# A hybrid decoder layer on one core: keys' products over all rows, a later planned end of the conditioning's sums, 16x16 joins in four parts, and an earlier place for the RWKV output's weights

## The chip, the cores and the metric

The kernel runs on one core of one Trainium2 chip. The time is the device time of one execution in microseconds. The engines are named as in the profile: PE (TensorE, matrix products), DVE (VectorE), ACT (ScalarE), POOL (GpSimd) and SP (SyncE, which here issues most of the DMAs).

## The reference

One decoder layer in float32, D = 1024, 512 tokens, FF = 2816:

```python
for l in range(DEPTH):
    ada = (c @ w_ada[l] + b_ada[l])[:, None, :]
    sh1, sc1, gt1, sh2, sc2, gt2 = jnp.split(ada, 6, axis=-1)
    h = rms_norm(x, norm1_w[l]) * (1.0 + sc1) + sh1
    proj = h @ w_in[l]
    att_in, rwkv_in, gate_in = jnp.split(proj, [ATT_IN, ATT_IN + RWKV_IN], axis=-1)
    y_att = attention_mixer(att_in) @ w_att_out[l]
    y_rwkv = rwkv7_mixer(rwkv_in, ...) @ w_rwkv_out[l]
    g_att, g_rwkv = jnp.split(jax.nn.sigmoid(gate_in + b_gate[l]), N_BRANCHES, axis=-1)
    x = x + gt1 * ((g_att * y_att + g_rwkv * y_rwkv) @ w_o[l])
    h = rms_norm(x, norm2_w[l]) * (1.0 + sc2) + sh2
    x = x + gt2 * conv_ffn(h, w_up[l], conv_w[l], conv_b[l], w_down[l])
return rms_norm(x, norm_f_w)
```

`rwkv7_mixer` runs a recurrence over the tokens for each of 16 heads of 64 channels:

```python
def step(state, inp):
    r_t, w_t, k_t, v_t, aa_t, bb_t = inp
    sa = jnp.einsum('bhvk,bhk->bhv', state, aa_t)
    state = state * w_t[:, :, None, :] + sa[..., None] * bb_t[:, :, None, :] + v_t[..., None] * k_t[:, :, None, :]
    return state, jnp.einsum('bhvk,bhk->bhv', state, r_t)
```

## The kernel before, in words

**Number format.** Products of large matrices are made of three fp32r matmuls each (high by high, low by high, high by low halves). A weight block is loaded into a `raw` buffer by SP, cast by ACT into the high half (`whi`), and DVE subtracts it from the raw block for the low half (`wlo`). Nearly all of these matmuls are 128x512. The small products of the recurrence are plain fp32; the trace shows two records for each of them. All matmuls are issued by one helper at line 148.

**Two ways of ordering.** Up to the end of the recurrence, work is entered as tasks into a list scheduler (`Plan`, from line 47): each task has an engine, a planned time `us`, a planned `lag` until its result counts as there, a priority (smaller first) and room that it takes and gives. The plan is run while the kernel is built, and the order in which it starts the tasks is the order of instructions on each engine. So planned times decide only the order; the chip waits on semaphores for what is really ready. What follows (`rwkv_out`, `mix_out`, the FFN) stands in the order in which its code is written.

**Conditioning (lines 330 to 390).** `c @ w_ada` for the last four parts (gt1, sh2, sc2, gt2) is summed on DVE while PE computes the attention's projections: for each of eight row blocks SP loads 128x1024 weights into one of two `araw` buffers, and DVE multiplies by a column of c and adds to `acc` (line 347). After the eighth, PE adds over the partitions with the products `ada`: eight columns, or four pieces of 256.

**The recurrence (line 1060 on).** The heads are worked in four groups g of four heads (two pairs i), the tokens in chunks of C = 64, so there are NCH = 8 chunks for each group. Before the chain of a group, the inverse of each chunk's triangular matrix is made; for group 3 by `inverse16`, which works on 16x16 blocks: DVE makes their inverses, and PE joins two neighbours with two products (`half_pe(0)`, `half_pe(1)`, line 1679), each of 64 matmuls in 32x32 tiles of PE, and ACT copies each result (`half_out`). Then `chain(g)` (line 1745) goes through the chunks. On PE a chunk has `state` (tile `xy`: the old state `mbd` by `ar`, then the values `uv` by the matrices `gt`, the keys' products), `state_out` (tile `xo`), `solve` (`u`, from `xs`), `update` (`u` from `uv` and `bkt`), and `outs` (`xo` from `uv`). In a chunk of pair i, the 64 rows `R[i]` of `uv` hold that chunk's values; the rows `X[i]`, the other half, are filled by `solved`. The values are computed for two chunks at a time by `vals`: PE's `values` (centring, `u<-cen,v`) and two copies on ACT (`value`). The copies write only the rows and columns that hold values, the rest of a fresh `uv` is undefined until `solved`. There are two `uv` buffers. While the chain waits, PE works on tasks of lower priority: `pg` (branch gates), `pa` (attention output) and `pr` (first products of the RWKV output).

**Gates.** `early_gate(m)` computes one of the 16 gate blocks during or before the recurrence and stores it to DRAM; the blocks in `self.late` are computed later, as filling for the chain's waits.

**`rwkv_out` (line 2098).** Eight products `pr` of 24 matmuls follow each other (the first three had their first six row blocks done earlier). `first(3, ..)` and `first(4, ..)` load their weights into what will be the buffers of w_o's blocks 7 and 6. In each round m the kernel finishes product m, maybe loads a further block of RWKV output weights (`block`, appended to `ahead`), combines the gates, and loads block m of w_o (`load_wo`). Two `raw` buffers serve all these loads, and SP issues them in the order written.

Of the kernel before, what the change touches and what calls it, by code (L numbers as in the profile page):

```python
# [18 lines left out]
P = 128  # L19
# [109 lines left out]
class Layer:  # L129
# [198 lines left out]
    def ada_rest(self):  # L328
# [5 lines left out]
        for part, name in ((2, "gt1"), (3, "sh2"), (4, "sc2"), (5, "gt2")):  # L334
            d, prev = {}, None
            for k in range(KD):
                def load(k=k, d=d, part=part):
                    d["raw", k] = self.accp.tile([P, D], F32, tag="araw", name=self.n("araw"), bufs=2)
                    nc.sync.dma_start(d["raw", k], self.w_ada[0][k * P : (k + 1) * P, part * D : (part + 1) * D])

                def step(k=k, d=d):
                    raw, ck = d["raw", k], self.col["c"][:, k : k + 1]
                    if k == 0:
                        d["acc"] = self.accp.tile([P, D], F32, tag="acc", name=self.n("acc"), bufs=2)
                        nc.vector.tensor_scalar(d["acc"], raw, ck, 0.0, op0=ALU.mult, op1=ALU.add)
                    else:
                        nc.vector.scalar_tensor_tensor(d["acc"], raw, ck, d["acc"], op0=ALU.mult, op1=ALU.add)  # L347
                prio = W_ + self.bodies
                t = pl.add("DMA", 1.6, load, [self.wide], prio, take=("araw2",), lag=2.2, name="ada")
                prev = pl.add("DVE", 1.3 if k else 0.75, step, [t, prev], prio, take=() if k else ("acc2",),  # L350
                              give=("araw2",), name="ada")
                yield
# [688 lines left out]
    def rwkv(self, tail):  # L1041
# [32 lines left out]
        for g in range(4):  # L1074
# [3 lines left out]
            self.chain(g)  # L1078
        self.late = range(6, KD)
        for m in range(2 * KD):  # L1080
# [496 lines left out]
    def inverse16(self, g):  # L1577
# [100 lines left out]

        def half_pe(j):

            if j == 0:
                d["pe"] = self.cps.tile([P, 512], F32, tag="t", name=self.n("pe"))
            for y in range(16):
                for e, b, x in quads:
# [31 lines left out]
        for j in range(2):  # L1716
            t = pl.add("PE", 2.6, lambda j=j: half_pe(j), [t, ey], 0.5, take=() if j else ("t",), name="pe")
            tc = t = sca(0.42, lambda j=j: half_out(j), [t], 0.5, name="pe")
# [26 lines left out]
    def chain(self, g):  # L1745
# [18 lines left out]
        def values(c):  # L1764

            for n, i, x in ((0, 0, 0), (0, 1, 0), (1, 1, 1), (1, 0, 1)):
                r = 64 * (i ^ x)
                self.mm(d["u"][r : r + 64, n * P : n * P + P], prs[i]["v"][:, (c + x) * C : (c + x + 1) * C], self.cen,
                        n == 0, n == 1)

        def value(c, x):
            if x == 0:
                uvs[c] = cw.tile([P, 2, 256], F32, tag="uv", name=self.n("uv"), bufs=2)
            b = uvs[c].rearrange("p x (i n) -> p (x i) n", i=2)[64 * x : 64 * x + 64]
            nc.scalar.copy((b[:, 1:3] if x else b[:, 0:4:3]), d["u"][64 * x : 64 * x + 64, :].rearrange("p (i n) -> p i n", i=2))
# [7 lines left out]
        def vals(c):  # L1783
            t = pe(0.54, lambda: values(c), [start, last_uv])
            t = sca(0.38, lambda: value(c, 0), [t], C_, take=("uv",))
            uvd[c] = uvd[c + 1] = sca(0.38, lambda: value(c, 1), [t], C_)
        vals(0)
        for c in range(NCH):
# [9 lines left out]
            def state(c=c, s=s, gt=gt, R=R, X=X, ih=ih):  # L1798
# [4 lines left out]
                for i, h, cs, ci in ih:  # L1803
                    self.mm(xy[X[i], cs], gt(i, h, R[i], X[i]), s["uv"][R[i], ci], c == 0 and h == 0, h == 1)

# [43 lines left out]

            st = pe(0.6 if c else 0.33, state, [uvd[c], start] + mb, take=("xy",), name=f"xy{g}.{c}")  # L1850
            so_ = pe(0.33 if c else 0.0, state_out, [st], C_ + 0.01, take=("xo",), name="xo")
            x = sca(0.29, xs, [st], take=("xs",), give=("xy",))
# [245 lines left out]
    def rwkv_out(self, mpool, wpool, psp):  # L2098
# [16 lines left out]
        for m in range(KD):  # L2115
            w, pr = [ahead[0][x] for x in ("w", "pm")]
            ahead.pop(0)
            prod(w, pr, range(late if m < 3 else 0, KD))
            if 2 < m < KD - 2:
                ahead.append(block(m + 2))  # L2120
            t = self.tr_[m]
# [283 lines left out]
```

## Time and profile before

| what | value |
|---|---|
| runs (us) | 1217.01, 1217.9, 1211.57; median 1217.01 |
| profiled execution (us) | 1212.94 |
| its span (us) | 1211.2 |
| mean granted TensorE clock | 0.993 |
| PE busy, instructions | 97% of the span, 7456 matmul records |
| moved by DMA | 138.39 MB, 114 GB/s |

The span runs from the first to the last record; 1.74 us of the execution lie outside of it. The rest of the kernel by time: the norm and the first loads up to 40 us, the projections for attention and its conditioning sums to about 215 us, attention, the remaining projections and the recurrence to about 758 us, `rwkv_out` and `mix_out` to about 846 us, the FFN to the end. A matmul that stands behind another is pipelined, so the length of its record is longer than the distance to the next start; where a time per matmul is wanted, the difference of two starts is read.

### The profile page before, as it was taken

To read this page: it belongs to the slowest core of one execution; us is meant where nothing else is said; L and a number is where in the kernel's file an instruction comes from. 1 tells how busy PE (TensorE), PEld (TensorE's weight loads), DVE (VectorE), ACT (ScalarE), POOL (GpSimd) and SP (SyncE) were. 2 spreads that over 40 slices of the span, in tenths; PEclk is the share of its full clock that TensorE was granted. 3 is DMA by queue.
4 is the path that set the end of the run, shared out by engine and by line. 5 is a ranking of instruction groups with operands and counts; after the bars stand their busy time and mean duration, and the time that the engine had idled before them with its cause. 6 is when DMAs were issued, how large, how long until landed. Compare 5 with 4: busy or idle time off the path is not lost.

```text
span 1211.2 us, 18982 instructions
## 1 busy us (share of the span) xinstructions
PE 1170.6 (97%) x7456; PEld 945.9 (78%) x7456; DVE 737.5 (61%) x1248; ACT 542.3 (45%) x1014; POOL 108.6 (9%) x228
## 2 busy tenths in 40 slices
PE   4999998999999999999999999999999999999997
PEld 3788887889777776767787667788888888888886
DVE  5688862431668986855797564764566665652235
ACT  4475521622565555364636453444444444441223
POOL 4000000000000103122102222003000000000001
PEclk9999999999999999999999999999999999999999
DMA  9845871130143342422332335460233333332331
GB/s 316 257 131 171 280 223 56 53 91 18 23 135 95 83 115 78 122 74 75 87 97 86 117 94 159 155 209 18 70 97 94 104 88 105 89 117 93 103 122 70
DMA packets 168040, 138.39 MB, mean 114 GB/s; under 512 B 8753, under 2 KB 150155, under 8 KB 167951
## 3 DMA queue, kind: packets, MB, share of 16 engines
q1 hardware_dynamic: 167807, 136.93, 37.2%
q8 instruction: 58, 0.95, 0.3%
q14 instruction: 31, 0.25, 0.1%
q10 hardware_dynamic: 144, 0.26, 0.1%
HBM read 127.13 MB, written 10.04 MB: 113 GB/s over the span
## 4 chain that ended last, share of the span: by engine, by line
PE 81%; DVE 8%; DMA 6%; ACT 2%; issue 2%; SPq 0%; POOL 0%; POOLq 0%; DVEq 0%; ACTq 0%
PE u L148 22%; PE o L148 13%; PE v L148 7%; PE pg L148 7%; PE qk L148 6%; PE r L148 3%; DMA araw<-in_w_ada_dram 3%; PE k L148 3%; PE pa L148 2%; PE early L148 2%; PE po L148 2%; PE xy L148 2%; PE pr L148 2%; PE xo L148 2%; PE pt L151 1%
## 5 line engine op out<-in xcount | busy, mean ns | idle before, releaser
L194 DVE TENSOR_TENSOR wlo<-raw,whi 128x1024 fp32r<-128x1024 f32 x65 | 79.6, 1225 | 141.1 <-ACT whi L193 141.1
L148 PE MATMUL u<-h2hi,whi 128*128 128x512 f32 (+2 forms) x368 | 140.6, 382 | 0.0
L148 PE MATMUL u<-h2lo,whi 128*128 128x512 f32 (+2 forms) x368 | 140.6, 382 | 0.0
L148 PE MATMUL u<-h2hi,wlo 128*128 128x512 f32 (+2 forms) x368 | 140.5, 382 | 0.0
L1141 ACT CAST whi<-raw 128x1024 fp32r<-128x1024 f32 (+2 forms) x73 | 72.6, 994 | 119.6 <-PE qk L148 45.5
L193 ACT CAST whi<-raw 128x1024 fp32r<-128x1024 f32 x65 | 68.5, 1054 | 97.3 <-PE o L148 53.7
L1144 DVE TENSOR_TENSOR wlo<-raw,whi 128x1024 fp32r<-128x1024 f32 (+2 forms) x73 | 83.7, 1148 | 19.5 <-ACT whi L1141 19.3
L148 PEld LDWEIGHTS u<-h2hi,wlo 128*128 128x128 f32 x368 | 69.1, 188 | 13.2
L148 PEld LDWEIGHTS u<-h2hi,whi 128*128 128x128 f32 x368 | 69.1, 188 | 13.2
L148 PEld LDWEIGHTS u<-h2lo,whi 128*128 128x128 f32 x368 | 69.1, 188 | 13.2 <-POOL h2lo L405 0.2
L2231 DVE SCALAR_TENSOR_TENSOR u<-u,cols,u 128x511 f32<-128x511 f32 x88 | 65.7, 746 | 4.5 <-ACT u L2229 3.0
L148 PE MATMUL qk<-hhi,wlo 128*128 128x512 f32 x160 | 64.0, 400 | 0.0
L148 PE MATMUL qk<-hhi,whi 128*128 128x512 f32 x160 | 63.6, 398 | 0.0
L148 PE MATMUL qk<-hlo,whi 128*128 128x512 f32 x160 | 63.6, 397 | 0.0
L148 PE MATMUL o<-whi,fhi 128*128 128x512 f32 x144 | 56.1, 390 | 0.3 <-DVE u L2231 0.3
L148 PE MATMUL o<-whi,flo 128*128 128x512 f32 x144 | 56.0, 389 | 0.0
L148 PE MATMUL o<-wlo,fhi 128*128 128x512 f32 x144 | 56.0, 389 | 0.0
L148 PE MATMUL pg<-hlo,whi 128*128 128x512 f32 x128 | 52.0, 406 | 0.0
L148 PE MATMUL pg<-hhi,whi 128*128 128x512 f32 x128 | 51.6, 403 | 0.0
L148 PE MATMUL pg<-hhi,wlo 128*128 128x512 f32 x128 | 51.5, 403 | 0.0
L810 DVE CUSTOM_DVE_ANT_0 sm<-sc,m 128x256 f32<-128x256 f32 (+1 forms) x64 | 23.9, 404 | 37.6 <-PE sc L148 36.5
L347 DVE SCALAR_TENSOR_TENSOR acc<-araw,cols,acc 128x1024 f32<-128x1024 f32 x28 | 35.9, 1281 | 17.3 <-DMA araw<-in_w_ada_dram 17.1
(450 smaller groups left out, 2761.3 us busy)
## 6 DMA issues: line engine op xcount, KB each, us to landing
raw<-in_w_in_dram SPq DMA_DIRECT2D x62, 512.0 KB
raw<-in_w_up_dram SPq DMA_DIRECT2D x44, 512.0 KB
araw<-in_w_ada_dram SPq DMA_DIRECT2D x32, 512.0 KB
raw<-in_w_down_dram SPq DMA_DIRECT2D x22, 512.0 KB
araw<-in_w_ada_dram SPq DMA_DIRECT2D x32, 256.0 KB
wvraw<-in_w_in_dram SPq DMA_DIRECT2D x20, 256.0 KB
raw<-in_w_rwkv_out_dram SPq DMA_DIRECT2D x8, 512.0 KB
raw<-in_w_o_dram SPq DMA_DIRECT2D x8, 512.0 KB
```

The lines of the kernel that those rows point to most:

```text
L148: return self.nc.tensor.matmul(out, lhsT, rhs, start=start, stop=stop)
L151: self.nc.tensor.matmul(out, in_, self.ident[: in_.shape[0], : in_.shape[0]], is_transpose=True, start=start, stop=stop,)
L193: self.nc.scalar.copy(hl[0], raw)
L194: (lo_eng or self.nc.vector).tensor_tensor(hl[1], raw, hl[0], op=ALU.subtract)
L347: nc.vector.scalar_tensor_tensor(d["acc"], raw, ck, d["acc"], op0=ALU.mult, op1=ALU.add)
L810: nc.vector.tensor_tensor_reduce(d["sm", h][:, :wd], d["sc"][h][:, :wd], m[:, 256 - wd : 256] if gi == 0 else m[:, :wd], 1.0, 3.0e38, op0= ...
L1141: nc.scalar.copy(d["w"][0], d["raw"])
L1144: nc.vector.tensor_tensor(d["w"][1], d["raw"], d["w"][0], op=ALU.subtract)
L2231: nc.vector.scalar_tensor_tensor(u[:, d:], pu[:, : S - d], ch(c), u[:, d:], op0=ALU.mult, op1=ALU.add)
```

## The change

There are five edits.

1. *Keys' products.* In `state` the product of `gt` and `uv` is taken over all 128 rows instead of the 64 rows `R[i]`. The rows `X[i]` of `uv` must be zero then, so a new function `zero` clears those parts of a fresh `uv` on POOL, planned at 0.6 us, and the copy of the values waits for it. The planned times of `state` and `state_out` are 0.5 and 0.24 instead of 0.6 and 0.33.
2. *Sums.* The eighth step of each of the four conditioning sums gets a planned lag of 3 us.
3. *Gates.* `self.late` begins at 7 instead of 6: gate 6 becomes an early gate.
4. *Joins.* `half_pe(j)` becomes four tasks `half_pe(j, q)` of 16 matmuls each, planned at 0.45 us with a lag of 0.4, instead of one task planned at 2.6.
5. *RWKV output's weights.* In `rwkv_out`, blocks 5, 6 and 7 are loaded in rounds 1, 2 and 3 instead of 3, 4 and 5.

```diff
                 prev = pl.add("DVE", 1.3 if k else 0.75, step, [t, prev], prio, take=() if k else ("acc2",),
-                              give=("araw2",), name="ada")
+                              give=("araw2",), lag=3.0 if k == KD - 1 else 0.0, name="ada")
...
-        self.late = range(6, KD)
+        self.late = range(7, KD)
...
-        def half_pe(j):
-
-            if j == 0:
+        def half_pe(j, q):
+
+            if j + q == 0:
                 d["pe"] = self.cps.tile([P, 512], F32, tag="t", name=self.n("pe"))
-            for y in range(16):
+            for y in range(4 * q, 4 * q + 4):
...
         for j in range(2):
-            t = pl.add("PE", 2.6, lambda j=j: half_pe(j), [t, ey], 0.5, take=() if j else ("t",), name="pe")
+            for q in range(4):
+                t = pl.add("PE", 0.45, lambda j=j, q=q: half_pe(j, q), [t, ey], 0.5, take=() if j + q else ("t",), lag=0.4, name="pe")
             tc = t = sca(0.42, lambda j=j: half_out(j), [t], 0.5, name="pe")
...
+        def zero(c):
+
+            uvs[c] = cw.tile([P, 2, 256], F32, tag="uv", name=self.n("uv"), bufs=2)
+            for x in range(2):
+                b = uvs[c].rearrange("p x (i n) -> p (x i) n", i=2)[64 * x : 64 * x + 64]
+                nc.gpsimd.memset((b[:, 0:4:3] if x else b[:, 1:3]), 0.0)
+
         def value(c, x):
-            if x == 0:
-                uvs[c] = cw.tile([P, 2, 256], F32, tag="uv", name=self.n("uv"), bufs=2)
...
-            t = sca(0.38, lambda: value(c, 0), [t], C_, take=("uv",))
+            z = pl.add("POOL", 0.6, lambda: zero(c), [start], C_, take=("uv",))
+            t = sca(0.38, lambda: value(c, 0), [t, z], C_)
...
-                    self.mm(xy[X[i], cs], gt(i, h, R[i], X[i]), s["uv"][R[i], ci], c == 0 and h == 0, h == 1)
+                    self.mm(xy[X[i], cs], gt(i, h, slice(0, P), X[i]), s["uv"][:, ci], c == 0 and h == 0, h == 1)
...
-            st = pe(0.6 if c else 0.33, state, [uvd[c], start] + mb, take=("xy",), name=f"xy{g}.{c}")
-            so_ = pe(0.33 if c else 0.0, state_out, [st], C_ + 0.01, take=("xo",), name="xo")
+            st = pe(0.5 if c else 0.33, state, [uvd[c], start] + mb, take=("xy",), name=f"xy{g}.{c}")
+            so_ = pe(0.24 if c else 0.0, state_out, [st], C_ + 0.01, take=("xo",), name="xo")
...
-            if 2 < m < KD - 2:
-                ahead.append(block(m + 2))
+            if 0 < m < KD - 4:
+                ahead.append(block(m + 4))
```

How the plan's order moves is seen at three places. The first is PE at the joins of group 3, where the 64 matmuls of `half_pe(0)` (`pe<-lr,gt 32x16`) and of `half_pe(1)` (`pe<-lt,lr 32x16`) stand among the chain of group 2; a row shows how often it repeats. Before:

```order
L148 MATMUL pa_1204_6722<-a03_6506,whi_1197_6661 128x512
L148 MATMUL u_1130_6223<-uv_1202_6709,bkt_918_4971 64x64 x2
L148 MATMUL u_1130_6223<-uv_1202_6709,bkt_1016_5507 64x64 x2
L148 MATMUL xo_1209_6739<-uv_1202_6709,gt_967_5237 64x64 x4
L148 MATMUL pe_1215_6779<-lr_1170_6428,gt_1085_5842 32x16 x64
L148 MATMUL xy_1217_6851<-mbd0_84,ar_916_4969 64x128
L148 MATMUL xy_1217_6851<-mbd1_85,ar_1014_5505 64x128
L148 MATMUL xy_1217_6851<-uv_1202_6709,gt_967_5237 64x64 x4
L148 MATMUL xo_1218_6859<-mbd0_84,ar_916_4969 64x128
L148 MATMUL xo_1218_6859<-mbd1_85,ar_1014_5505 64x128
L148 MATMUL pe_1215_6779<-lt_1171_6429,lr_1170_6428 32x16 x64
L148 MATMUL u_1130_6223<-xs_1219_6862,gt_967_5237 64x64 x4
```

After, from the first part of `half_pe(0)` to the second task of `half_pe(1)`:

```order
L148 MATMUL pe_1202_6747<-lr_1175_6478,gt_1091_5927 32x16 x16
L148 MATMUL u_1129_6241<-xs_1203_6764,gt_968_5255 64x64 x4
L148 MATMUL pe_1202_6747<-lr_1175_6478,gt_1091_5927 32x16 x32
L148 MATMUL u_1129_6241<-uv_1183_6554,bkt_916_4975 64x64 x2
L148 MATMUL u_1129_6241<-uv_1183_6554,bkt_1012_5504 64x64 x2
L148 MATMUL xo_1201_6743<-uv_1183_6554,gt_968_5255 64x64 x4
L148 MATMUL pe_1202_6747<-lr_1175_6478,gt_1091_5927 32x16 x16
L148 MATMUL xy_1211_6854<-mbd0_84,ar_914_4973 64x128
L148 MATMUL xy_1211_6854<-mbd1_85,ar_1010_5502 64x128
L148 MATMUL xy_1211_6854<-uv_1183_6554,gt_968_5255 64x64 x4
L148 MATMUL xo_1212_6864<-mbd0_84,ar_914_4973 64x128
L148 MATMUL xo_1212_6864<-mbd1_85,ar_1010_5502 64x128
```

The two solid blocks of 64 have become pieces of 16 and 32 between the chain's steps; behind the rows shown, `half_pe(1)` goes on as 16, 32 and 16 with `u` and `xo` of the chain and one `pa` between them, and the wide `pa` products that stood between the chain's steps ahead of the joins now stand behind them.

The second place is PE where it makes `ada` of the last part, gt2, among the products of the attention's values (`v`). Before:

```order
L148 MATMUL v_376_1888<-wvhi_240_1319,hhi_93 128x512
L148 MATMUL v_376_1888<-wvhi_240_1319,hlo_94 128x512
L148 MATMUL ada_380_1900<-acc_353_1750,few_65 1x256
L148 MATMUL ada_381_1902<-acc_353_1750,few_65 1x256
L148 MATMUL v_376_1888<-wvlo_238_1317,hhi_93 128x512
```

After:

```order
L148 MATMUL v_382_1947<-wvhi_239_1316,hlo_94 128x512
L148 MATMUL v_382_1947<-wvlo_237_1314,hhi_93 128x512
L148 MATMUL ada_384_1957<-acc_358_1784,few_65 1x256
L148 MATMUL ada_385_1959<-acc_358_1784,few_65 1x256
L148 MATMUL v_382_1947<-wvhi_245_1346,hhi_93 128x512
```

They stand in the second of two value tiles instead of the first, 49 rows further on in PE's order; those of gt1, sh2 and sc2 are moved by 12, 33 and 36 records. On SP, one `raw` load of 512 KB more stands ahead of the last `araw` load.

The third place is SP in `rwkv_out`: its loads of RWKV output weights and of w_o. Before:

```order
L178 DMA raw_1332_7693<-in_w_o_dram 128x1024
L178 DMA raw_1333_7709<-in_w_o_dram 128x1024
L178 DMA raw_1334_7725<-in_w_o_dram 128x1024
L178 DMA raw_1335_7753<-in_w_rwkv_out_dram 128x8x128
L178 DMA raw_1339_7766<-in_w_o_dram 128x1024
L178 DMA raw_1340_7794<-in_w_rwkv_out_dram 128x8x128
L178 DMA raw_1344_7807<-in_w_o_dram 128x1024
L178 DMA raw_1345_7835<-in_w_rwkv_out_dram 128x8x128
```

After:

```order
L178 DMA raw_1333_7729<-in_w_o_dram 128x1024
L178 DMA raw_1334_7739<-in_w_rwkv_out_dram 128x8x128
L178 DMA raw_1338_7752<-in_w_o_dram 128x1024
L178 DMA raw_1339_7762<-in_w_rwkv_out_dram 128x8x128
L178 DMA raw_1343_7775<-in_w_o_dram 128x1024
L178 DMA raw_1344_7803<-in_w_rwkv_out_dram 128x8x128
L178 DMA raw_1348_7816<-in_w_o_dram 128x1024
L178 DMA raw_1349_7850<-in_w_o_dram 128x1024
```

Blocks 5, 6 and 7 of the RWKV output's weights have moved from the fourth, sixth and eighth place of eleven to the second, fourth and sixth; the loads of w_o fill the other places in the same order as before, and DVE and ACT split the blocks in this order too.

## The prediction

> **What bounds the kernel now.** I read the page first, then the waits of PE, then the granted clock in short windows, and last the timeline at each place that the change touches.
>
> ```profile
> PE 1170.6 (97%) x7456; PEld 945.9 (78%) x7456; DVE 737.5 (61%) x1248; ACT 542.3 (45%) x1014; POOL 108.6 (9%) x228
> ...
> q8 instruction: 58, 0.95, 0.3%
> ...
> PE 81%; DVE 8%; DMA 6%; ACT 2%; issue 2%; SPq 0%; POOL 0%; POOLq 0%; DVEq 0%; ACTq 0%
> ```
>
> PE is busy for 97% of the span and has 81% of the chain that ended last. It works in order, so the time changes where PE's own work gets shorter or where it stops waiting; a wait of another engine counts only if PE stands behind it. The waits of PE, as groups (total, times, longest), hold three that the change can reach, the third with a row of its own for the lower halves:
>
> ```profile
> PE ada L148 <- DVE acc L347: 3.3, 1, 3.3
> ...
> PE u L148 <- issue: 2.2, 1, 2.2
> ...
> PE pr L148 <- ACT whi L193: 1.6, 1, 1.6
> ...
> PE pr L148 <- DVE wlo L194: 0.8, 2, 0.5
> ```
>
> They cost more than they say. The windows view (stretch, busy PE with its records, granted clock, DMA share, GB/s) shows a stretch of 3.4 us at half clock behind each of them:
>
> ```profile
> 147.10:150.50 3.40, 2.67 (x16) 1.00 0.94 280
> 184.70:188.10 3.40, 1.19 (x5) 1.00 0.55 154
> 188.10:191.50 3.40, 3.40 (x8) 0.50 0.38 99
> 689.90:693.30 3.40, 1.21 (x71) 1.00 0.02 5
> 693.30:696.70 3.40, 3.40 (x45) 0.50 0.02 5
> 771.80:775.20 3.40, 1.27 (x5) 1.00 0.50 158
> 775.20:778.60 3.40, 3.40 (x9) 0.50 0.51 154
> ```
>
> Where PE was busy for about 1.2 of 3.4 us, the next 3.4 us ran at 0.50, which loses 3.4 x 0.5 = 1.7 us. Where it was busy for 2.67, as at 147.1, the clock stayed at 1.00 (150 to 175 us are at 1.00 too). So each of the three waits is worth its length and 1.7 us.
>
> **The change part by part.** *Keys' products.* PE's timeline around one chunk of the recurrence, and one place with products over 128 rows (x counts records, two for each fp32 matmul):
>
> ```profile
> 675.66 0.44 PE L148 MATMUL xy<-mbd,ar 128*64 128x128 f32 x4
> 676.03 0.45 PE L148 MATMUL xy<-uv,gt 64*64 64x64 f32 x8
> 676.40 0.44 PE L148 MATMUL xo<-mbd,ar 128*64 128x128 f32 x4
> 676.77 0.50 PE L148 MATMUL pg<-hlo,whi 128*128 128x512 f32 x1
> ...
> 679.42 0.45 PE L148 MATMUL u<-uv,bkt 128*64 128x64 f32 x8
> 679.70 0.61 PE L148 MATMUL u<-cen,v 128*64 128x128 f32 x8
> 680.14 0.40 PE L148 MATMUL xo<-uv,gt 128*64 128x64 f32 x8
> ```
>
> The starts tell the price of a change of shape. Eight records of 128x64 followed by the same shape take 679.70 - 679.42 = 0.28 us; eight of 64x64 between two other shapes take 676.40 - 676.03 = 0.37. So 0.09 goes with leaving the 64*64 shape. Eight records of 128x128 take 680.14 - 679.70 = 0.44, so four would take 0.22 to 0.27 (with the fixed part of a group), and before the 64*64 shape they take 0.37: 0.10 to 0.15. After the change the three groups have one shape, and both switches go: 0.19 to 0.24 for a chunk. Chunk 0 of a group has no product with the state and keeps its switches; 7 chunks in each of 4 groups give 28 x 0.19 = 5.3 us, at most 6.7, and 0 if the switch isn't the cause. The product itself, over 128 rows in place of 64, is the same eight records; both shapes run at about 0.28.
>
> The Trainium skill speaks against this step: "TensorEngine Tiling (Array Packing)", section Performance Considerations, recommends row tiling by two where the contraction is 64, which the 64x64 shape does here. By that rule the eight records would take twice as long over 128 rows, and the step would cost time; the trace has 0.28 us for eight over 128 rows, so it does not agree here.
>
> What is added is two memsets on POOL for each of the 16 pairs of chunks, and a wait of ACT's copy of the values for them. The nearest rows:
>
> ```profile
> L1975 POOL TENSOR_TENSOR var<-var,few 128x4 f32<-128x4 f32 x16 | 16.2, 1014 | 1.3
> ...
> L1498 POOL MEMSET tt<- 128x512 f32 x3 | 1.6, 526 | 6.1 <-DVE lt L1478 6.1
> ```
>
> A memset of 128x512 takes 0.53 us, and two of 64 x 256 at most as much each. POOL is busy for 9%. The zeros need only a free uv buffer, of which there are two, and a buffer comes free about two chunks before its copy. I cost them at nothing, with POOL's idle time as cover; the case without cover is a rival below.
>
> *Sums of the conditioning.* PE waits at its first product of gt2:
>
> ```profile
> L347 DVE SCALAR_TENSOR_TENSOR acc<-araw,cols,acc x4: 1283/1284/1285, 177.6 to 185.6; 128x1024 f32<-128x1024 f32 x4
> ```
> ```profile
> 181.00 0.39 PE L148 MATMUL qk<-hlo,whi 128*128 128x512 f32 x1
> 181.23 0.39 PE L148 MATMUL qk<-hhi,wlo 128*128 128x512 f32 x1
> ...
> 183.22 0.39 PE L148 MATMUL v<-wvhi,hlo 128*128 128x512 f32 x1
> 186.91 1.02 PE L148 MATMUL ada<-acc,few 128*1 128x256 f32 x4 [3.30 <-DVE acc L347]
> ```
>
> A 128x512 matmul comes every 0.23 us, so 186.91 - 183.22 - 0.23 = 3.46 us are lost, and 1.7 with the half clock: 5.2. The last sum starts at 185.6 and ends at 186.9. In the new order, this product stands 49 rows of PE further on, nearly all of 0.23 us: 11 us. On SP one more weight load stands ahead of the last load of the sum; the sums come (185.6 - 177.6) / 3 = 2.7 us apart, each with its load, so I take 2.7 us for it. The sum is then ready at 189.6, and PE arrives at 183.4 + 11 = 194.4. The wait goes, with some 5 us in hand. DVE and SP do the same work. Gain 4.9, from 0 (the sums slip as far as PE does) to 5.2. The other edit of the plan, gate 6 in the early gates, moves 24 matmuls from the end of the recurrence to before it, and adds one store and one load of a tile. PE's work is the same, and 128x512 matmuls still stand between nearly all chain steps of the last groups: nothing, within 1.5 us either way, which is also the size of the small waits (0.8, 0.8 and 0.4 us) that a new plan deals out anew.
>
> *Joins.* PE's timeline of group 3 before:
>
> ```profile
> 686.31 1.26 PE L148 MATMUL pe<-lr,gt 32*32 32x16 f32 x128
> 687.50 0.44 PE L148 MATMUL xy<-mbd,ar 128*64 128x128 f32 x4
> ...
> 689.17 1.26 PE L148 MATMUL pe<-lt,lr 32*32 32x16 f32 x128 [0.48 <-issue]
> 692.62 0.45 PE L148 MATMUL u<-xs,gt 64*64 64x64 f32 x8 [2.19 <-issue]
> 693.00 0.58 PE L148 MATMUL pa<-a,whi 128*128 128x512 f32 x1
> ```
>
> The traffic of the DMA queues from 684 to 702 us, in 40 slices of 0.45 us:
>
> ```profile
> GB/s 0 92 215 248 27 0 36 0 0 0 0 0 0 36 0 0 0 0 0 0 0 36 0 0 0 0 0 0 41 159 259 314 355 37 0 0 36 0 85 254
> ...
> q8 instruction: 4, 0.07, 1.6%
> ```
>
> Both idle times are "issue": no data was late. The four marks of 36 are the four instruction packets, at about 686.7, 689.9, 693.5 and 700.2. PE has 2 x 7456 instructions (matmul and load) and the page 58 packets, 257 for each. So a packet of 256 came every 3.3 us at best. A join is 64 matmuls with 256 instructions for 1.2 us of work, so instructions are what PE waits for, 2.67 us, and the half clock behind it costs 1.7.
>
> After the change, the joins stand in parts between chain steps. But no 128x512 matmul stands between the first and the last part except one. Between them are 128 join matmuls and 28 small ones of the chain, at four instructions each 624, over two packets: 6.7 us or more. Their work is 687.50 - 686.31 = 1.19 twice for the joins, 0.37 x 3 for xy and xo, some 2.1 for the other chain steps, and 0.6 for four more changes of shape at 0.10 to 0.15: 6.2 us. About 0.5 of the 2.67 us stays, and 0.6 goes to the switches: 1.5 is gained, and since PE is then busy for nine tenths, perhaps the 1.7 as well. Bounds: -1.0 (all waits stay, more switches) and 4.4 (all go). I take 2.0, a little over the middle.
>
> *Output weights.* The end of product 4 and the start of product 5 of rwkv_out, PE first, then ACT and DVE:
>
> ```profile
> 771.71 0.39 PE L148 MATMUL pr<-yhi,w 128*128 128x512 f32 x1
> 773.70 0.50 PE L148 MATMUL pr<-yhi,whi 128*128 128x512 f32 x1 [1.60 <-ACT whi L193]
> ```
> ```profile
> 766.44 1.05 ACT L1983 CAST wohi<-raw 128x1024 fp32r<-128x1024 f32 x1 [0.47 <-DMA raw<-in_w_o_dram]
> ...
> 772.60 1.04 ACT L193 CAST whi<-raw 128x1024 fp32r<-128x1024 f32 x1 [1.25 <-DMA raw<-in_w_rwkv_out_dram]
> ```
> ```profile
> 795.12 1.22 DVE L1984 TENSOR_TENSOR wolo<-raw,wohi 128x1024 fp32r<-128x1024 f32 x1
> ```
>
> The weights come through two raw buffers. The rows are those of wo1 and block 5, with wo2 between them: a weight every 3.1 us. Block 5 is fourth in the row, behind wo0, wo1 and wo2. Lost are 773.70 - 771.71 - 0.23 = 1.76 for its high half, 0.8 for low halves (two waits, in the list above) and 1.7 with the half clock: 4.3. Afterwards block 5 is second: its high half starts at about 766.4, its low half is done by 769, and PE needs it at 771.9. Blocks 6 and 7 are fourth and sixth, ready at about 775 and 781, needed at 777 and 783. What is late next would be wo3 to wo7, which now end the row. The row is eleven blocks long as before and ends with DVE's wo7 at 795.12 + 1.22 = 796.3; PE starts product 5 at 771.9, has 72 matmuls of 0.23 for products 5 to 7 and then six of `o` for each wo, so it needs wo7 at 771.9 + 114 x 0.23 = 798.1. Only 1.8 us are left. Gain 4.3, at least 2.3 if wo7 is late by 2 us.
>
> **Sum.** 5.3 + 4.9 + 2.0 + 4.3 = 16.5 us. The profiled execution took 1212.94 us (1.74 around its span of 1211.2): 1212.94 - 16.5 = 1196.4. The median of the three runs, 1217.01, lies 4.07 above it. I can't tell which of the two the next runs follow, and add half of it: **1198 us**. A measurement tells 0.5% of this kernel, 6.1 us, from no change.
>
> **The rivals.** *Waits only move.* The plan is drawn anew up to the recurrence's end, and a new order may stop PE elsewhere; in rwkv_out wo7 may replace block 5. Then only the keys' 5.3 and little else stays: 1212.94 - 5.3 + 2 = 1210. For it speaks that the plan's times aren't the chip's (it planned no wait of 3.3 us at 183); against it, 5 us in hand at the sums.
>
> *The keys' products get dearer.* If eight records over 128 rows cost double, 28 x 0.28 = 7.8 us are added and the switches' 5.3 gained: 1198 + 7.8 = 1206. Row 679.42 speaks against it. That is the result by the skill's rule on row tiling.
>
> *Slower: ACT waits for POOL's zeros.* A norm's step on POOL (1.01 us by its row) and the two memsets (2 x 0.53 at most) can stand ahead of the copy. If each of the 16 pairs of chunks were late by 2.07 us with nothing left for PE to do, 33 us would be added: 1198 + 33 = 1231. It decides from 16.5 / 16 = 1.03 us uncovered each, or half of the pairs. Against it: two buffers, and matmuls of other stages to fill with.
>
> *The joins aren't parted from each other.* In the new order they have hardly any wide matmuls between them, so instructions may starve PE as before, half clock included: the 2.0 goes and 1.0 for the switches is added, 1198 + 3.0 = 1201.
>
> **How the numbers follow.** Forecast 0.60 (1192 to 1204: all upper bounds, and the losses of wo7 and small waits), joins as before 0.14 (1201), waits only move 0.15 (1210, half of it within 0.5%), dearer products 0.05 (1206), slower 0.06 (1231). The low end is 1212.94 less 20.6, the sum of the upper bounds (6.7, 5.2, 4.4, 4.3), and less 1.5 for small waits, so 1191; the high end 1210 takes in half of the moved waits. Below 1210.9 lies 0.84, within 0.5% 0.10, above 0.06.
>
> **What would show it.** Keys: the step from xy<-mbd to the next wide matmul falls from 1.11 to about 0.92. Sums: no wait of ada for acc, and no half clock near 188. Joins: "issue" below 1 us in all, and full clock behind it. Weights: no wait of pr for whi, and `o` not waiting for wolo. I am wrong if a wait over 2 us stands at a new place, if u's copy on ACT waits for POOL, or if eight xy<-uv records take over 0.35.

## The result and the profile after

| | before | after |
|---|---|---|
| first comparison, median (us) | 1216.70 (6 runs) | 1200.90 (6 runs, 1198.07 to 1809.12) |
| ratio, 95% interval | | 0.9868 (0.984 to 0.9896) |
| second comparison (run e1_after), median (us) | 1213.07 (23 runs) | 1197.44 (5 runs, 1197.23 to 1200.33) |
| ratio, 95% interval | | 0.9878 (0.9855 to 0.9901) |
| mean granted clock, second comparison | 0.9895 | 0.9944 |

The changed kernel is 15.6 to 15.8 us faster; forecast were 1198 us and a sum of 16.5. The run of 1809.12 us was at a low clock from start to end, 0.587 in the mean, and as it was the profiled one, the profile after is that of the second comparison, an execution of 1200.33 us; one run of e2_late6 below took 6437.77 us, and neither of the two is in a ratio. First its page, with the lines that answer to those of before:

```profile
span 1198.6 us, 19059 instructions
...
PE 1164.2 (97%) x7456; PEld 948.9 (79%) x7456; DVE 739.1 (62%) x1248; ACT 542.5 (45%) x1014; POOL 113.9 (10%) x260
...
PE 86%; DVE 7%; DMA 3%; ACT 2%; issue 1%; SPq 0%; POOL 0%; POOLq 0%; DVEq 0%; ACTq 0%
```

PE has as many records as before, is busy for 6.4 us less (1170.6 - 1164.2), and takes more of the chain. Of the waits shown before, these were `ada` for acc (3.3), `pr` for whi (1.6) and for wlo (0.8), and two on issue (2.2 and 0.5). The list of PE's waits now has none of the first three, and one on issue:

```profile
PE pe L148 <- issue: 2.1, 1, 2.1
```

The windows, at the places that answer to those of before (stretch, busy PE with its records, clock, DMA share, GB/s):

```profile
185.00:188.40 3.40, 3.40 (x16) 1.00 0.67 200
188.40:191.80 3.40, 3.40 (x17) 1.00 0.03 7
336.00:339.40 3.40, 2.42 (x16) 1.00 0.56 161
339.40:342.80 3.40, 3.40 (x10) 0.50 0.14 39
680.80:684.20 3.40, 1.42 (x58) 0.99 0.64 193
684.20:687.60 3.40, 3.31 (x22) 0.50 0.72 226
771.80:775.20 3.40, 3.40 (x16) 1.00 0.46 165
```

The half clock at 188 and at 775 is gone, with the waits ahead of it. The one behind the joins is there as before (now at 684), and one is new at 339.

Where the time went is read from three marks on PE: the first chunk of the chain that uses a state, the last transposes of the recurrence, and the first `o`. Before:

```profile
451.12 0.44 PE L148 MATMUL xy<-mbd,ar 128*64 128x128 f32 x4
...
752.92 0.63 PE L151 MATMUL t<-ident,yt 128*128 128x128 f32 x4
...
793.11 0.39 PE L148 MATMUL o<-wohi,mhi 128*128 128x512 f32 x1
```

After:

```profile
445.55 0.44 PE L148 MATMUL xy<-mbd,ar 128*64 128x128 f32 x4
...
745.58 0.63 PE L151 MATMUL t<-ident,yt 128*128 128x128 f32 x4
...
780.47 0.39 PE L148 MATMUL o<-wohi,mhi 128*128 128x512 f32 x1
```

Up to the chain 5.6 us were gained (451.12 - 445.55), in the four chains 1.8 (301.80 against 300.03 us from the first mark to the second), and from the end of the recurrence to the first `o` 5.3 (40.19 against 34.89). That is 12.6 us, the difference of the two profiled executions; what follows takes the same time in both. Both have the same mean clock, 0.993, so a gain by the clock is not in these 12.6 us.

### The profile page after: what moved, and what is told of

It is laid out like the page before. It is cut to its first block, busy times and chain, and to the rows that moved or that the text cites. A ratio compares the mean times of both kernels' runs of the same rounds, so it can differ in the third digit from the quotient of the medians.

```text
span 1807.4 us, 19059 instructions
## 1 busy us (share of the span) xinstructions
PE 1780.9 (99%) x7456; PEld 1163.1 (64%) x7456; DVE 741.5 (41%) x1248; ACT 545.5 (30%) x1014; POOL 113.2 (6%) x260
## 4 chain that ended last, share of the span: by engine, by line
PE 98%; DVE 1%; DMA 0%; issue 0%; ACT 0%; SPq 0%; POOLq 0%; POOL 0%; DVEq 0%; ACTq 0%
PE u L148 22%; PE o L148 14%; PE qk L148 10%; PE v L148 10%; PE pg L148 10%; PE r L148 4%; PE k L148 4%; PE pr L148 4%; PE pa L148 3%; PE po L148 2%; PE early L148 2%; PE pt L151 2%; PE sc L148 2%; PE xy L148 1%; PE xo L148 1%; PE lg L148 1%
## 5 line engine op out<-in xcount | busy, mean ns | idle before, releaser
L148 PE MATMUL u<-h2hi,whi 128*128 128x512 f32 (+2 forms) x368 | 185.5, 504 | 0.0
L148 PE MATMUL u<-h2lo,whi 128*128 128x512 f32 (+2 forms) x368 | 184.6, 502 | 0.0
L148 PE MATMUL u<-h2hi,wlo 128*128 128x512 f32 (+2 forms) x368 | 184.5, 501 | 0.0
L148 PE MATMUL qk<-hlo,whi 128*128 128x512 f32 x160 | 93.8, 586 | 0.0
L148 PE MATMUL qk<-hhi,whi 128*128 128x512 f32 x160 | 93.4, 584 | 0.0
L148 PE MATMUL qk<-hhi,wlo 128*128 128x512 f32 x160 | 92.2, 576 | 0.0
L148 PE MATMUL pg<-hhi,whi 128*128 128x512 f32 x128 | 73.5, 574 | 0.0
L148 PE MATMUL pg<-hhi,wlo 128*128 128x512 f32 x128 | 73.0, 570 | 0.0
L148 PE MATMUL pg<-hlo,whi 128*128 128x512 f32 x128 | 73.0, 570 | 0.0
L148 PEld LDWEIGHTS po<-v,pts 128*128 128x128 f32 x240 | 48.0, 266 | 6.7 <-issue 1.9
```

What stands on the lines that cost most here:

```text
L148: return self.nc.tensor.matmul(out, lhsT, rhs, start=start, stop=stop)
```

## The experiments

All were run beside the kernel before on the same chip. Three chips served: one for the first four runs, one for the next four, one for the last four. The interval of a ratio is 0.13 to 0.26% to either side, some 1.6 to 3.2 us, so smaller steps are read from the traces. The ratio is not the quotient of the two medians and differs from it by up to 1.5 us; differences in the text are those of the medians.

| run | what it is | median (us) | before (us) | ratio, 95% interval |
|---|---|---|---|---|
| e1_after | the change | 1197.44 | 1213.07 | 0.9878 (0.9855 to 0.9901) |
| e2_late6 | the change, gate 6 late | 1202.62 | 1213.07 | 0.9908 (0.9886 to 0.993) |
| e3_keys | keys alone | 1212.98 | 1213.07 | 0.999 (0.9969 to 1.0012) |
| e4_joins | joins alone | 1215.90 | 1213.07 | 1.0023 (1.0008 to 1.0038) |
| e5_rw | weights alone | 1209.14 | 1212.33 | 0.9966 (0.995 to 0.9982) |
| e6_keys_rw | keys and weights | 1207.81 | 1212.33 | 0.9957 (0.9941 to 0.9973) |
| e7_ada | sums alone | 1209.62 | 1212.33 | 0.9971 (0.9958 to 0.9985) |
| e8_joins1 | the change, joins in two pieces | 1198.41 | 1212.33 | 0.9885 (0.9859 to 0.9911) |
| e9_keys0 | the change without keys | 1202.46 | 1213.84 | 0.9912 (0.9895 to 0.9929) |
| e10_rw0 | the change without weights | 1205.27 | 1213.84 | 0.9942 (0.9919 to 0.9965) |
| e11_ada0 | the change without sums | 1205.07 | 1213.84 | 0.9931 (0.9911 to 0.9951) |
| e12_three | keys, sums and weights only | 1200.73 | 1213.84 | 0.989 (0.9866 to 0.9914) |

**e1_after.** No edit.

> The changed kernel again, for a trace at full clock. Theory (four terms: 5.3 + 4.9 + 2.0 + 4.3 us): about 16 us under before; no wait of ada for acc, none of pr for whi, half clock gone near 188 and 775; the two waits on issue at the 16x16 joins (2.67 us before) at 0.5 to 1.2 us, because no wide matmul stands between the parts. Rival 'waits only move': about 5 us under before where nothing else disturbs, with a new wait over 2 us at some other place; the gain of 16 would then have to come from somewhere that the prediction doesn't name.

The four waits did as said, but for the joins. Their timeline on PE in this run:

```profile
679.61 0.44 PE L148 MATMUL pe<-lt,lr 32*32 32x16 f32 x32
679.98 0.45 PE L148 MATMUL u<-xs,gt 64*64 64x64 f32 x8
680.36 0.73 PE L148 MATMUL pe<-lt,lr 32*32 32x16 f32 x64
681.01 0.53 PE L148 MATMUL xo<-uv,gt 128*64 128x64 f32 x8
681.47 0.49 PE L148 MATMUL pa<-a,whi 128*128 128x512 f32 x1
681.90 0.33 PE L148 MATMUL pe<-lt,lr 32*32 32x16 f32 x17
684.29 0.41 PE L148 MATMUL pe<-lt,lr 32*32 32x16 f32 x15 [2.07 <-issue]
```

PE stops on issue in the middle of the last part (after 17 of its 32 records), and waits 2.07 us instead of 2.67 before.

**e2_late6.**

```diff
-        self.late = range(7, KD)
+        self.late = range(6, KD)
```

> The changed kernel with gate 6 put back among the late gates (self.late = range(6, KD)). The plan then puts one to six wide pa matmuls between nearly all parts of the joins. Theory (PE starves for instructions there): the waits on issue near the joins go to under 0.3 us and no half clock follows; 0.5 to 3 us under the changed kernel. Rival (gate 6 costs nothing and fills nothing, joins are no longer limited by instructions): the same within 0.5 us, and waits on issue alike in both traces.

The waits on issue are gone, as the theory has it: PE's list of waits has none on issue at all, and the clock is full around the joins. But the kernel is 5.2 us slower than the changed one on the same chip (2.5 us in the two profiled executions), not 0.5 to 3 faster. The end of the recurrence shows why:

```profile
746.82 0.63 PE L151 MATMUL t<-ident,yt 128*128 128x128 f32 x4 [1.06 <-DVE y L1945]
749.46 0.74 PE L148 MATMUL pr<-yhi,whi 128*128 128x512 f32 x2 [2.02 <-ACT yhi L2084]
```
```profile
747.60:751.00 3.40, 1.37 (x5) 1.00 0.00 0
751.00:754.40 3.40, 3.40 (x10) 0.50 0.00 0
```

PE has nothing left to do when the last y is awaited: 774 wide matmuls stand between the first and the last mark of the recurrence where the changed kernel has 761. The wait of the joins has become one of 2.02 and one of 1.06 us at the end, with its own half clock behind.

**e3_keys.** Edit 1 of the change alone.

```diff
...
-            t = sca(0.38, lambda: value(c, 0), [t], C_, take=("uv",))
+            z = pl.add("POOL", 0.6, lambda: zero(c), [start], C_, take=("uv",))
+            t = sca(0.38, lambda: value(c, 0), [t, z], C_)
...
-                    self.mm(xy[X[i], cs], gt(i, h, R[i], X[i]), s["uv"][R[i], ci], c == 0 and h == 0, h == 1)
+                    self.mm(xy[X[i], cs], gt(i, h, slice(0, P), X[i]), s["uv"][:, ci], c == 0 and h == 0, h == 1)
...
```

> Before with the keys' products over 128 rows and the zeros alone; PE's order is that of before row for row. Theory (two changes of shape less in 28 chunks): 5.3 us under before, at most 6.7; the step from xy<-mbd to the next wide matmul 0.92 instead of 1.11 us, the four stalls as before. Rival 'dearer products': eight records of xy<-uv take 0.56 instead of 0.28, 2.5 us over before. Rival 'ACT waits for POOL': steps as in the theory, but waits of ACT for POOL's memset and 5 us or more over before.

The expectation was wrong in saying that PE's order is that of before: with the new planned times and the zeros as tasks, 12 more wide matmuls (128x512) came to stand between the first mark and the last transposes (771 against 759). The products did get cheaper (see the run of keys and weights), and PE reached the first `pr<-yhi,w` 4.5 us sooner (747.70 against 752.16). But the first `o` came at 793.39, and at 793.11 before. PE's waits and ACT's split of block 5:

```profile
PE pr L148 <- ACT whi L193: 3.8, 2, 2.7
...
PE pr L148 <- ACT yhi L2083: 1.3, 1, 1.3
```
```profile
771.69 1.04 ACT L193 CAST whi<-raw 128x1024 fp32r<-128x1024 f32 x1 [1.58 <-DMA raw<-in_w_rwkv_out_dram]
```

Block 5 was 0.9 us sooner than before (772.60), and the end of the recurrence 1.2 (752.04 against 753.27 for the last record of the transposes). From the first mark to the second this execution is no shorter than before's (451.12 to 752.92, here 449.46 to 751.69). Two things stand against the cheaper products there: the 12 wide matmuls, at 0.23 us each 2.8 us, and two more windows at half clock behind the joins (three in a row from 687.6 on), 3.4 us. Behind the second mark the 12 matmuls are missing, and PE waits instead: 3.8 us for `whi` and 1.3 for `yhi`, where before has 1.6 and none. Neither rival holds: eight records of xy<-uv don't take 0.56, and ACT has no wait for a memset of uv in the list of its waits.

**e4_joins.** Edit 4 alone.

```diff
...
-            t = pl.add("PE", 2.6, lambda j=j: half_pe(j), [t, ey], 0.5, take=() if j else ("t",), name="pe")
+            for q in range(4):
+                t = pl.add("PE", 0.45, lambda j=j, q=q: half_pe(j, q), [t, ey], 0.5, take=() if j + q else ("t",), lag=0.4, name="pe")
```

> Before with the 16x16 joins in four parts alone; in this plan one to six wide pa matmuls stand between the parts. Theory: no wait on issue over 0.3 us near the joins and no half clock behind, 2.7 + 1.7 us gained less 0.6 for more changes of shape: 3 to 4 us under before. Rival (more changes of shape take back what the parts gain, the instructions come no sooner): within 1 us of before.

No wait on issue and full clock at the joins, as the theory has it. Yet nothing is gained: 0.08 to 0.38% slower than before. PE waits later:

```profile
756.27 0.74 PE L148 MATMUL pr<-yhi,whi 128*128 128x512 f32 x2 [2.01 <-ACT yhi L2078]
...
774.21 0.50 PE L148 MATMUL pr<-yhi,whi 128*128 128x512 f32 x1 [2.19 <-ACT whi L193]
```

The second wait was 1.60 in before; the first is new. Here 15 more wide matmuls than in before stand between the two marks (774 against 759), and they are missing behind, where PE waits. The rival was nearer in time (2.8 us over before, and it allowed 1) and wrong about the cause: the instructions do come in time, and the gain goes to a later wait. Why the kernel comes out slower than before, and not even with it, is not shown.

**e5_rw.** Edit 5 alone.

```diff
-            if 2 < m < KD - 2:
-                ahead.append(block(m + 2))
+            if 0 < m < KD - 4:
+                ahead.append(block(m + 4))
```

> Before with the earlier place of the RWKV output's weights alone; all else, the plan included, as before. Theory: the wait of pr for whi and wlo and the half clock near 775 go: 4.3 us under before, and the distance from the last transposes of the recurrence to the first o falls from 39.8 to about 35 us. Rival (a wait at wo7 takes its place): waits of o for wohi or wolo of 2 us or more, 2 us under before at most.

As the theory has it, PE waits for no weights in rwkv_out, and from the first `pr<-yhi,w` to the first `o` the profile has 4.9 us less (755.40 to 791.49, against 752.16 to 793.11). The measured median is 3.2 us under before. In the profiled execution 3.4 us were lost again at the joins, where three windows at half clock follow each other instead of one:

```profile
689.00:692.40 3.40, 1.26 (x128) 1.00 0.02 5
692.40:695.80 3.40, 2.41 (x12) 0.50 0.02 5
695.80:699.20 3.40, 3.40 (x75) 0.50 0.25 69
699.20:702.60 3.40, 3.40 (x21) 0.50 0.23 85
702.60:706.00 3.40, 3.22 (x67) 1.00 0.41 118
```

**e6_keys_rw.** Edits 1 and 5.

> Before with the keys' products over 128 rows and the earlier place of the weights together. Theory (the cheaper keys' products are real, 0.30 us in each of 28 chunks, but alone they only make PE reach the late weights of block 5 sooner): with the weights there in time they count in full, 4.3 + 8.3 = 12 us under before, at least 8, and 5 to 8 under the kernel with the weights alone. Rival (the keys' products gain nothing that lasts, whatever the weights): as the kernel with the weights alone within 1.5 us.

1.3 us under the kernel with the weights alone: the rival's number. The trace says more. Summed over the recurrence, from each start to the next and with half-clock time counted at half, the records of xy and of the first xo take 28.0 us here and 34.3 with the weights alone, 6.3 less; they take 33.7 in before and 27.5 with keys alone, 6.2 less. So the products are cheaper in every kernel that has the edit. But PE again runs out of work at the recurrence's end (at 756.78 it has waited 1.30 us for `yhi`), and the 12 wide matmuls that moved ahead are then missing behind.

**e7_ada.** Edit 2 alone.

```diff
...
-                              give=("araw2",), name="ada")
+                              give=("araw2",), lag=3.0 if k == KD - 1 else 0.0, name="ada")
```

> Before with the lag of 3 us for the last conditioning sums alone. Theory: no wait of ada for acc, no half clock near 188, 4.9 us under before; the recurrence starts and ends 5 us sooner, so the weights of block 5, which follow its end, come 5 us sooner too and nothing is given back. Rival (given back at the weights as with the keys' products): a wait of pr for whi of 5 us or more, and the first o within 1 us of before.

The wait and its half clock are gone; the chain starts 6.6 us sooner (444.56), and the profiled execution ends 4.9 us sooner. The median is 2.7 us under before. Block 5 comes 4.8 us sooner (767.83 against 772.60), as expected. What is given back lies between the first and the second mark: 303.38 us (444.56 to 747.94) against 301.80, as two windows at half clock follow the joins here instead of one, another 1.7 us. Behind the second mark the first `o` comes 40.30 us later, and 40.19 in before: the waits of `pr` are longer (1.8 us for `whi`, and 1.6 in three for low halves, against 1.6 and 0.8 in two), but no half clock follows them.

**e8_joins1.** Edit 4 taken out of the changed kernel.

> The changed kernel with the joins of group 3 in two pieces again instead of eight. Theory after the first runs (in the changed kernel the parts have hardly a wide matmul between them, 2.1 us of issue and a half clock are still there): within 1.5 us of the changed kernel, with waits on issue of 2 to 3 us in the trace. Rival (the prediction's 2.0 us for the parts): 2 us or more over the changed kernel, with a longer wait on issue.

1198.41 against 1212.33, so 13.9 us under before where the changed kernel has 15.6; by the intervals they can't be told apart. Waits on issue are 1.6 us here and 2.1 in the changed kernel, where the rival has them longer. That the parts are worth 2 us is not shown.

**e9_keys0, e10_rw0, e11_ada0.** The changed kernel without edit 1, 5 or 2.

> The changed kernel without its first edit (keys' products over 64 rows again, no zeros, the old planned times). Theory (the cheaper chain steps, 0.30 us in 28 chunks by the trace, count in full where the weights come in time and PE has work up to the chain's end): 5.3 us over the changed kernel by the prediction, 8.3 by the measured step. Rival (as between the kernel with weights alone and that with keys and weights: the chain's waits on other engines and a worse place for the fillers take most of it back): 1 to 2 us over the changed kernel, with waits of pr for yhi absent here.

> The changed kernel without the earlier place of the RWKV output's weights. Theory (block 5's weights come about 20 us after the chain's end whatever PE does, and the first o some 40 us after it, as in before): the first o 5.3 us later, waits of pr for whi and wlo of 4 us or more, and 5 us over the changed kernel or more. Rival (the other edits have made room for the weights): within 2 us of the changed kernel.

> The changed kernel without the lag of 3 us. Theory: the wait of ada for acc (2 to 3 us) is back, 3 to 5 us over the changed kernel. Rival (the half clock near 188 comes and goes by itself and the wait alone is small): 2 to 3 us over it, as the median of the kernel with the lag alone stood to before (2.7).

They stand 11.4, 8.6 and 8.8 us under before, where the changed kernel stands 15.6 under it: keys are worth 4.3 us in the changed kernel, the earlier weights 7.1 and the lag 6.9, each with some 3.5 us of uncertainty. Without the weights' edit, the waits for them are back:

```profile
PE pr L148 <- ACT whi L193: 1.8, 2, 1.6
...
PE pr L148 <- DVE wlo L194: 1.1, 2, 0.5
```

and without the lag the wait for the sums:

```profile
PE ada L148 <- DVE acc L347: 2.5, 1, 2.5
```

For weights and lag the theory holds in the main: the first `o` is 4.4 us later without the weights' edit (expected were 5.3, and waits of 4 us where the list has 2.9) and 4.2 later without the lag. For the keys 4.3 is nearer to the prediction's 5.3 than to the rival's 1 to 2, but the uncertainty takes in both. It is not the products' gain alone either: without this edit the plan puts wide matmuls between the later parts of the joins, and there PE has no wait on issue and the full clock, so this kernel saves at the joins part of what it loses by the products.

**e12_three.** Edits 1, 2 and 5; joins and gate 6 as before.

> Before with three of the five edits: keys' products, lag of the sums, earlier weights; the joins in two pieces and gate 6 late as in before. Theory (parts of the joins gain nothing without wide matmuls between them; gate 6 among the late gates moves fillers into the chain's middle, so that PE waits for yhi at its end): 3 to 5 us over the changed kernel, with waits of pr for yhi. Rival (joins and gate 6 are both worth nothing): within 1.5 us of the changed kernel, and perhaps under it.

13.1 us under before, so 2.5 over the changed kernel, and the intervals overlap: between the two expectations, and open. Its list of PE's waits has:

```profile
PE pe L148 <- issue: 2.0, 1, 2.0
...
PE pr L148 <- ACT yhi L2083: 1.3, 1, 1.3
```

The profiled execution, 1194.91 us, is the fastest of the six. Its wait on issue, from 679.1 to 681.07, falls into two stretches, and neither is followed by half clock:

```profile
676.60:680.00 3.40, 2.50 (x151) 1.00 0.29 83
680.00:683.40 3.40, 2.33 (x35) 1.00 0.03 6
683.40:686.80 3.40, 3.40 (x102) 1.00 0.48 154
```

No kernel was found that clearly beats the changed one.

## Why the prediction held, step by step

*What bounds it.* PE in its order, with waits that cost their length and often a half clock: right. Where a wait went and nothing later was late, the time went with it. That each wait costs 1.7 us more was too strict: behind the waits on issue at the joins one window at half clock followed in before and in the changed kernel, three in e5, and none in e12.

*Keys, 5.3 us.* Mechanism right; the size is about right, in part by luck, as two errors in it offset each other. The records of these products take 6.2 us less with keys alone and 4.9 less in the changed kernel (28.8 against 33.7 in before); leaving the edit out costs 4.3. The step of one chunk shows both errors. In the changed kernel, a chunk 1 and a chunk 2:

```profile
445.55 0.44 PE L148 MATMUL xy<-mbd,ar 128*64 128x128 f32 x4
445.82 0.40 PE L148 MATMUL xy<-uv,gt 128*64 128x64 f32 x8
446.05 0.39 PE L148 MATMUL xo<-mbd,ar 128*64 128x128 f32 x4
446.37 0.66 PE L151 MATMUL pt<-ident,bk 128*128 128x128 f32 x4
...
450.83 0.44 PE L148 MATMUL xy<-mbd,ar 128*64 128x128 f32 x4
451.10 0.55 PE L148 MATMUL xy<-uv,gt 128*64 128x64 f32 x8
451.49 0.44 PE L148 MATMUL xo<-mbd,ar 128*64 128x128 f32 x4
451.86 0.50 PE L148 MATMUL t<-sg0h,g2h 128*128 128x512 f32 x1
```

Chunk 1 takes 0.82 us instead of 1.11, more than the 0.92 predicted: both switches together cost 0.30, not 0.19. Chunk 2 takes 1.03. Its values are copied by ACT at that moment, until 450.39 + 0.76 = 451.15:

```profile
450.39 0.76 ACT L1781 COPY uv<-u 64x256 f32<-64x256 f32 x2 [0.66 <-DVE mbd L1844]
```

In most even chunks the faster chain meets that copy, and the step is 0.98 to 1.14 us. Sixteen odd chunks at 0.30 and twelve even ones at 0.1 would be 6.0 us, an estimate; the prediction had 28 at 0.19. The advice of the Trainium skill ("TensorEngine Tiling (Array Packing)", section Performance Considerations) to tile the rows by two for a contraction of 64 is not borne out here: eight records take 0.23 us over 128 rows (446.05 - 445.82) and took 0.37 between two switches in 64x64. What a long run of 64x64 products takes, without the switches, no run here shows. What the prediction cost at nothing, the zeros, cost nothing:

```profile
L1777 POOL MEMSET uv<- 64x256 f32 x32 | 9.8, 306 | 35.7 <-PE xo L148 34.6
```

They take 9.8 us of POOL, which waits for `xo` of the pair of chunks that had the buffer; no wait of ACT for them is listed.

*Sums, 4.9 us.* Right: 5.6 us at the chain's start in the traces, 6.9 by leaving it out, 2.7 alone. The order put the product behind the sum, with no wait left: the last sum of gt2 starts at 188.4 and takes 1.28, so it is there at 189.7 (189.6 was forecast), and PE comes to its product at 195.97 (194.4).

*Gate 6, nothing.* Wrong where the joins are in parts, in the step "PE's work is the same, and 128x512 matmuls still stand between nearly all chain steps". Two things follow from this edit in the plan. With gate 6 late the joins get wide matmuls between them, with gate 6 early hardly any (e2 against e1; e9 has some all the same); and with gate 6 early fewer wide matmuls stand ahead of the recurrence's end, so that PE still has some when it waits for the last y. The second is worth more: e2 is 5.2 us slower. A wait of `pr` for yhi of 1.3 to 2.0 us stands in all kernels with gate 6 late that have cheaper keys or joins in parts (e2, e3, e4, e6, e12), and in none with gate 6 early (e1, e8, e9, e10, e11), nor in before, e5 and e7, where the chain is as slow as it was. Gate 6 alone was not run, but e8 and e12 differ in nothing else, with the joins in two pieces: they stand 13.9 and 13.1 us under before, and the intervals can't tell them apart. So the edit's worth hangs on the joins: 5.2 us with parts, and nothing that these runs show without them. The parts in turn, with gate 6 late, stand no better than two pieces (e2 10.5 us under before, e12 13.1).

*Joins, 2.0 us.* Wrong. The step was that of 2.67 us on issue 0.5 stays and the half clock perhaps goes. In the trace 2.07 us stay, the half clock stays, and all join records of the recurrence together take 12.2 us instead of 11.3, against 9.7 where wide matmuls stand between the parts (e2, e4). That wide matmuls between the parts take the wait away is shown by these two. That it is a wait for instructions is read from the four packets in the prediction's DMA row, and these runs fit it. The rival "not parted from each other" was right, and its 1.0 for the switches near the 0.9 found.

*Weights, 4.3 us.* Right: no wait, 5.3 us from the transposes to the first `o`; 3.2 alone, 7.1 by leaving it out. wo7, feared to be late, is not waited for.

*The sum.* 16.5 forecast against 15.6, in part by luck: the joins' 2.0 didn't come, and half clock fell by more than was summed. By their mean clocks the runs of before lose (1 - 0.9895) x 1213 = 12.7 us to it and those of the changed kernel (1 - 0.9944) x 1197 = 6.7, so at most 6 of the 15.6 us are clock (less where PE would have waited anyway). The prediction had 3.4 of that in the sums and the weights, and no more than a part of 1.7 in the joins. The two profiled executions, at the same clock, differ by 12.6 us; the prediction's keys, sums and weights without the half clock are 5.3 + 3.2 + 2.6 = 11.1.

*Terms don't add.* Single edits measured alone sum to -0.1 + 2.8 - 3.2 - 2.7 = -3.2 us without gate 6, and leaving them out of the whole gives 4.3 + 6.9 + 7.1 for three. Block 5's weights come 19.1 to 19.7 us after the last transposes in before, e3, e4 and e7 (753.27 to 772.60, 752.04 to 771.69, 753.98 to 773.11, 748.29 to 767.83), whatever PE has gained until then. An edit ahead of that point is worth its time only if the recurrence's end moves with it (the sums) or the weights are no longer waited for. The prediction's rival "waits only move" describes much of what the keys and the joins do alone.

## What to carry to other kernels

Where the next wait stands close behind, a saving alone measures as nothing; look up what is late next, and judge an edit inside the whole set (leave it out) as well as alone. Two things count in a plan of fillers: enough wide work between dense runs of small matmuls, and enough of it left for the last wait of the chain. Edits that share the fillers, as joins and gate 6 do here, are judged together. A product over half of the rows is not worth a change of PE's tile shape when the neighbours have another: zeros in the other half were cheaper here.

## What the runs showed of the hardware

Half clock comes in stretches of 3.4 us that keep to a grid: in before they begin at 188.1, 693.3 and 775.2, which are 148 and 24 times 3.41 us apart. Such a stretch doesn't need a gap in PE's records ahead of it. In the changed kernel 2.42 of 3.40 us busy were followed by 0.50 (at 339), whereas in before 2.67 were not (at 147); and in e11_ada0 it follows a stretch that the records fill:

```profile
136.10:139.50 3.40, 3.40 (x32) 1.00 0.98 289
139.50:142.90 3.40, 3.40 (x14) 0.50 1.01 358
```
```profile
136.67 1.90 PE L148 MATMUL ada<-few,acc 128*128 128x1 f32 x16
```

Half of these 32 records have one column and take about 0.11 us each, where a 128x512 record takes 0.23; in the stretch ahead of 339 eight have two columns. So the profile's busy time counts narrow products like wide ones, and it does not decide alone about the clock; what does is not shown by these runs. The half clock can also last: in e5_rw three stretches follow one with 1.26 us busy, although PE's records, 64 of 75 of them in 32x32 tiles, fill the second one. The Trainium skill ("TensorE: Matmul & The Clock Gate", section What's actually happening) has the clock go down after an idle window of about 3.4 us, and up again after a busy one; the length of the window agrees with the rows, but here it went down behind windows with 1.2 to 2.4 us of records, and at 699 in e5_rw it had not come up behind one that records fill. By the mean clocks, the number of such stretches differs from run to run of the same kernel: the runs with keys alone are at 1207.4 to 1208.6 us with clocks of 0.993 and 0.994 in four cases, and at 1211.8 to 1217.4 with 0.986 to 0.989 in eight. A profile is one draw of these: before's had 0.993, where its runs have 0.9895 in the mean.
